# Half of a kernel's attention-probability tiles transposed as 32x32 blocks on VectorE and regrouped through DRAM

## The chip, the cores and the metric

The kernel runs on one core of one Trainium2 chip. The metric is the device time of one execution in microseconds (us). A core has a matrix engine (TensorE, in the profile PE, with its weight loads shown as PEld), VectorE (DVE), ScalarE (ACT), GpSimd (POOL) and SyncE (SP), which here only issues transfers (DMAs). Each engine executes its own instructions strictly in the order in which they stand in the program, and an instruction that waits for another engine holds back everything behind it on its own engine.

## The reference

A two-layer encoder trunk over 1024 tokens of width 1024, in float32. Layer 0 mixes with differential attention (8 heads, each the difference of two softmaxes of 64-wide queries and keys), layer 1 with latent attention (8 heads, scores from a 128-wide and a 64-wide part). Cut to what matters:

```python
# layer 0, per block of 128 queries
sc = jnp.einsum('bqhcd,bkhcd->bhcqk', qb, k) * scale
p = jax.nn.softmax(sc, axis=-1)
p = p[:, :, 0] - lam * p[:, :, 1]
o = jnp.einsum('bhqk,bkhd->bqhd', p, v)
# layer 1
sc = (einsum('bqhd,bkhd->bhqk', qn, k_nope) + einsum('bqhr,bkr->bhqk', qp, k_pe)) * scale
p = jax.nn.softmax(sc, axis=-1)
o = einsum('bhqk,bkhd->bqhd', p, v)
```

Around it stand an RMS norm, a conditioning shift, scale and gate, input projections, a SiLU gate, an output projection and a residual. The changed kernel computes the same.

## The kernel before

**Precision.** Every matrix product is made of three TensorE products (`mm3`, lines 186 to 188): an operand is split into a rounded part (`...h`, a cast on ACT) and the rest (`...l`, a subtraction on DVE or POOL), and the products high x high, high x low and low x high are added.

**Attention.** A head has 1024 queries, taken as 8 tiles of 128 queries; below, tiles are numbered from the start of a layer, 8 to a head. For one tile:

- Layer 0 (`q_tile`, L873): scores `s` of 128x1024 for c=0 and again for c=1, four matmuls of 128x512 each, into one of two PSUM buffers: c=0 always gets one of them, c=1 the other. `softmax_part` takes the row maximum on DVE (`nm`, L404) and the exponential on ACT (`e`, L406): for c=0 into a tile `e`, for c=1 in place. DVE then forms e0 + z*e1 (L879 to L881). Only after that is the buffer of c=1 free for the next tile.
- Layer 1 (`scores1`, L1703): ten matmuls of 128x512 into one of two buffers used in turn, `nm`, `e`. A buffer is free once its exponential is done.

The product with V needs the probabilities with the keys on the partitions, so each `e` is transposed: four TensorE transposes of 128x128 write one PSUM bank `tr` (L387), ACT rounds it into `pth` (L389), DVE writes the rest `ptl` (L390); twice per tile (kh = 0, 1). Two tiles t = 0, 1 form a query pair `qp`, four pairs to a head. When both are transposed, 24 matmuls of 128x256 (`pv`) add up the output of the pair. `after_scores` and the class `Tail` set the program order: a tile's first half is transposed after the scores of the next tile, its second half among the scores of the one after that, and `pv` follows there.

**Filling.** Between these pieces stand steps of other work for TensorE (`acc`): one step is three matmuls of 128x512 of the projections that the next heads need. `FILL0` and `FILL1` say how many steps stand at each place. Their weights come through `wraw` (DMA), `wh` (ACT) and `wl` (POOL, L235); the rotated queries and keys through DMAs `rp_sw` and POOL (L331, L336, L350 to L359).

**What sets the order.** The program text is the wish; a scheduler places the instructions of each engine and moves one ahead of another where it holds that the other is not ready. What it made is fixed in the program, and the order listings below show it. All DMAs are issued by SP, in one queue.

Of the kernel before, what the change touches and what calls it, by code (L numbers as in the profile page):

```python
# [40 lines left out]
FILL0 = ((1, 2, 1, 1, 1, 0), (1, 1, 1, 1, 1, 1)) * 3 + ((1, 2, 1, 1, 1, 0), (1, 1, 1, 1, 1, 0))  # L41
FILL1 = ((1, 0, 1, 0), (0, 1, 0, 0)) * 4
# [49 lines left out]
def trunk(ctx: ExitStack, tc: tile.TileContext, A, out):  # L92
# [303 lines left out]
    def alloc_pt(ap_):  # L396
        pth = [ap_.tile([P, 4, 2 * P], F32R, name="pth", tag="pt", bufs=6) for _ in range(2)]
        ptl = [ap_.tile([P, 4, 2 * P], F32R, name="ptl", tag="pt", bufs=6) for _ in range(2)]
        return pth, ptl
# [463 lines left out]
    def q_tile(h, half, ti, zz, ep, mid=lambda i: None):  # L863
# [5 lines left out]
        for c in range(2):  # L869
# [4 lines left out]
            with tc.issue_after(combined[-1]) if c == 0 and combined else nullcontext():  # L874
                es.append(softmax_part(None if c else ep, s_ps, zs[c], 1 if ep is a0a else 3))
# [34 lines left out]
    def finish(o, y, l, h, half, dst, ap_, dgs):  # L910

        if dst is None:
            b, rb = bcast_rows(ap_, y, "osq", 4)
# [60 lines left out]
    class Tail:  # L974
# [12 lines left out]
        def pv(self, kh):  # L987
# [3 lines left out]
            if kh == 0:  # L991
                if qp == 0:
                    c["vt"] = load_v(c["pool"], c["l"], c["h"])
                if qp % 2 == 0:
                    c["o_"] = bank("pv", "pv")
                    c["open"](qp // 2)
# [4 lines left out]

    tails, hooks = [None, None], []

# [15 lines left out]
    def after_scores(fill, n):  # L1019

        prev, last = tails
        if last:
            last.turn(0)
        fill(n)
        if prev:
            prev.pv(0)
        fill(n + 1)
        new = hooks[:]
        if prev:
            prev.pv(1)  # L1030
        fill(n + 2)
        for f in new:
            hooks.remove(f)
            f()

    def attn0(h, fills, extra=None, late=None):
# [10 lines left out]
        ctx_ = dict(pool=a0b, l=0, h=h, open=lambda half: None, close=close)  # L1047
        for qp in range(4):
            half = qp // 2
            if qp % 2 == 0:  # L1050
                zz = first.pop(0) if first else sm.tile([P, 4], F32, name="zz")
            for t in range(2):
# [13 lines left out]
                if first:  # L1066
                    e0 = first.pop()
                else:
                    e0 = q_tile(h, half, (qp * 2 + t) % 4, zz, a0b, mid)
                    fill(2)  # L1070
                    after_scores(fill, 3)
                side.tick()
                tails[:] = [tails[1], Tail(qp, t, e0, zz, ctx_)]
# [171 lines left out]
    tail0 = attn0(NH - 1, lambda i: FILL7[i] if i < Z_LAST else (0,) * 6, extra0, late0)  # L1245
    mk.clear()
# [30 lines left out]
    def group0(gi, fulls):  # L1277
# [3 lines left out]
        def chunk(k):  # L1281
            if gi == 1:
                h1[k][1] = xt2k("h1h"), xt2k("h1l")
                h1f[k] = ut(f"h1f{k}", dt=F32)
# [19 lines left out]
    def ut(name, spare=False, dt=F32R):  # L1304
        return up.tile([P, HF], dt, name=name, tag="us" if spare else "u", bufs=4 if spare else 20)
# [4 lines left out]
    wp = pool(stw, "wp1", side="right")  # L1310
    stv = ExitStack()
# [31 lines left out]
    def combos():  # L1343
# [5 lines left out]
        for k in range(4):  # L1349
# [19 lines left out]
            split_t(3, k, t3_, (ut("t3h"), ut("t3l")))  # L1369
# [228 lines left out]
    cqput = lora(3, CQ, qag, QL, lambda: ut("cqr", dt=F32), lambda: ut("cq"), 1)  # L1598
# [88 lines left out]
    def scores1(h, half, ti, zz):  # L1687
# [18 lines left out]
        return softmax_part(ap, s_ps, zz[:, ti : ti + 1])  # L1706
# [3 lines left out]
    def attn1(h, fills, extra=None, late=None):  # L1710
# [14 lines left out]
        ctx_ = dict(pool=ap, l=1, h=h, open=open_, close=close)  # L1725
        for qp in range(4):
            half = qp // 2
            if qp % 2 == 0:
                zz = first1.pop(0) if first1 else sm.tile([P, 4], F32, name="zz1")
            for t in range(2):  # L1730
# [7 lines left out]
                if first1:  # L1738
                    e = first1.pop()
                else:  # L1740
                    e = scores1(h, half, ti, zz)
                    fill(0)
                    after_scores(fill, 1)
                tails[:] = [tails[1], Tail(qp, t, e, zz, ctx_)]
# [18 lines left out]
    for n, steps in V1_AT:  # L1763
        for tt in v1_left[:n]:
            v1_tile(tt, 1, ap, "pt", 6)
# [9 lines left out]
    for tt in v1_left:  # L1775
        v1_tile(tt, 1, ap, "pt", 6)
    stv.close()
    ap2 = pool(st5, "attn1b")
# [36 lines left out]
    tail1 = attn1(NH - 1, lambda i: (0, 0, 0, 0), extra1, late1)  # L1815
    mk.clear()
# [129 lines left out]
```

## Time and profile before

| | us |
|---|---|
| median of 3 runs | 1431.51 (1429.72 to 1432.22) |
| the profiled execution, its own time | 1429.47 |
| its span in the trace | 1427.7 |
| busy: PE, DVE, ACT, POOL | 1396.7, 903.3, 743.3, 603.7 |

The profiled execution took 1.8 us more than its span, and 2.0 us less than the median. The span runs from the first to the last recorded instruction. The granted TensorE clock was 0.997 over the run. Layer 0's attention lies at about 150 to 690 us, layer 1's at about 960 to 1340 us.

### The profile page before, as it was taken

How to read it: one execution, taken by the hardware profiler on the slowest of the kernel's cores; microseconds unless marked ns; L12 is line 12 of the kernel's file. 1: busy time of each engine (PE TensorE's matmuls, PEld its weight loads, DVE VectorE, ACT ScalarE, POOL GpSimd, SP SyncE). 2: the span in 40 equal slices, each digit the busy share in tenths (PEclk: the TensorE clock that was granted, in tenths of full speed). 3: DMA queues.
4: the chain of work that ended last, by engine and by line, in shares of the span. 5: the costliest groups of instructions: out<-in, count | busy, mean ns of one | idle time of the engine just before them, and what ended most of it. 6: DMA issues, size and time to landing. Idle time of an engine off the chain costs nothing.

```text
span 1427.7 us, 20748 instructions
## 1 busy us (share of the span) xinstructions
PE 1396.7 (98%) x7478; PEld 1167.8 (82%) x7478; DVE 903.3 (63%) x1366; ACT 743.3 (52%) x1318; POOL 603.7 (42%) x483
## 2 busy tenths in 40 slices
PE   9999899999999999998999999999999999999997
PEld 7778688888888887887788788887888888888886
DVE  7756786767777767677435876255566555555355
ACT  6623375666565656566343644345455454555442
POOL 4415164656464646453561244412241331413562
PEclk9999999999999999999999999999999999999999
DMA  9777723233332333236663132465334532336663
GB/s 350 252 231 231 243 69 95 84 103 82 96 98 88 94 92 89 89 96 224 240 200 125 52 104 82 146 191 167 113 115 115 135 101 81 99 96 215 217 209 138
DMA packets 128473, 201.64 MB, mean 141 GB/s; under 512 B 17777, under 2 KB 54769, under 8 KB 128370
## 3 DMA queue, kind: packets, MB, share of 16 engines
q1 hardware_dynamic: 128370, 200.31, 45.6%
q8 instruction: 59, 0.97, 0.3%
q14 instruction: 44, 0.36, 0.1%
HBM read 131.11 MB, written 45.55 MB: 124 GB/s over the span
## 4 chain that ended last, share of the span: by engine, by line
PE 80%; DVE 6%; DMA 5%; issue 3%; ACT 3%; POOL 2%; SPq 1%; ACTq 0%; POOLq 0%; DVEq 0%
PE s L1703 9%; PE acc L188 8%; PE acc L186 8%; PE acc L187 8%; PE tr L387 7%; PE s L873 7%; PE oacc L186 4%; PE oacc L188 4%; PE oacc L187 4%; PE pv L187 4%; PE pv L188 4%; PE pv L186 4%; DVE ada L444 2%; PE zacc L186 1%; PE zacc L188 1%
## 5 line engine op out<-in xcount | busy, mean ns | idle before, releaser
L389 ACT CAST pth<-tr 128x512 fp32r<-128x512 f32 x256 | 150.2, 587 | 280.4 <-PE tr L387 277.2
L404 DVE TENSOR_REDUCE nm<-s 128x1 f32<-128x1024 f32 x192 | 233.9, 1219 | 72.7 <-PE s L873 66.3
L390 DVE TENSOR_TENSOR ptl<-tr,pth 128x512 fp32r<-128x512 f32 x256 | 176.1, 688 | 136.6 <-ACT pth L389 136.1
L235 POOL TENSOR_TENSOR wl<-wraw,wh 128x512 fp32r<-128x512 f32 (+2 forms) x82 | 101.3, 1237 | 234.6 <-ACT wh L234 212.5
L387 PE MATMUL tr<-ident,e 128*128 128x128 f32 x1024 | 154.6, 273 | 4.4 <-DVE ptl L390 4.2
L387 PEld LDWEIGHTS tr<-ident,e 128*128 128x128 f32 x1024 | 120.7, 140 | 46.1 <-DVE ptl L390 22.6
L406 ACT ACTIVATE e<-s,nm 128x1024 f32<-128x1024 f32 x128 | 143.6, 1122 | 24.8 <-DVE nm L404 24.4
L186 PE MATMUL acc<-h0h,wh 128*128 128x512 f32 x360 | 151.2, 420 | 2.5 <-DVE v_hl L366 1.7
L186 PE MATMUL pv<-pth,vt 128*128 128x256 f32 x512 | 147.4, 288 | 0.0
L187 PE MATMUL pv<-ptl,vt 128*128 128x256 f32 x512 | 145.8, 285 | 0.0
L188 PE MATMUL pv<-pth,vt 128*128 128x256 f32 x512 | 144.7, 283 | 0.0
L188 PE MATMUL acc<-h0h,wl 128*128 128x512 f32 x360 | 142.9, 397 | 0.1
L187 PE MATMUL acc<-h0l,wh 128*128 128x512 f32 x360 | 142.0, 394 | 0.0
L1118 POOL TENSOR_TENSOR wol<-wor,woh 128x512 fp32r<-128x512 f32 x64 | 84.7, 1343 | 83.7 <-ACT woh L1117 79.5
L186 PEld LDWEIGHTS pv<-pth,vt 128*128 128x128 f32 x512 | 97.3, 190 | 3.1 <-ACT pth L389 0.5
L187 PEld LDWEIGHTS pv<-ptl,vt 128*128 128x128 f32 x512 | 97.5, 190 | 2.8
L188 PEld LDWEIGHTS pv<-pth,vt 128*128 128x128 f32 x512 | 97.7, 191 | 0.1
L873 PE MATMUL s<-ks,qa 128*128 128x512 f32 x256 | 82.7, 403 | 5.2 <-DVE e L881 2.7
L336 POOL TENSOR_TENSOR rp_sw<-rp_sw,sinT 128x512 f32<-128x512 f32 x42 | 55.3, 1316 | 71.1 <-DMA rp_sw<-rp_raw 69.5
L881 DVE SCALAR_TENSOR_TENSOR e<-s,z,e 128x1024 f32<-128x1024 f32 x64 | 82.1, 1283 | 2.1
L331 POOL TENSOR_TENSOR rp_r<-rp_raw,cosT 128x512 f32<-128x512 f32 x38 | 49.7, 1307 | 77.3 <-ACT rp_raw L326 44.0
L873 PE MATMUL s<-ks,qb 128*128 128x512 f32 x256 | 81.1, 396 | 0.5 <-DMA qb<-qb 0.5
(624 smaller groups left out, 3355.5 us busy)
## 6 DMA issues: line engine op xcount, KB each, us to landing
ada<-in_ada_ss SPq DMA_DIRECT2D x32, 512.0 KB, 6.8
wraw<-in_w_s SPq DMA_DIRECT2D x64, 256.0 KB, 2.8
vS<-v_hl SPq DMA_DIRECT2D x32, 512.0 KB, 4.8
vt<-vS SPq DMA_DIRECT2D x32, 512.0 KB, 4.5
wor<-in_w_out SPq DMA_DIRECT2D x64, 256.0 KB, 3.5
rp_sw<-rp_raw SPq DMA_DIRECT2D x168, 64.0 KB, 2.0
bc_s<-bc_d SPq DMA_DIRECT2D x30, 256.0 KB, 4.2
oS<-bc_s SPq DMA_DIRECT2D x30, 256.0 KB, 2.6
```

Of the source, the lines that this page charges most:

```text
L186: PE.matmul(psum, ah, bh, start=first, stop=False)
L187: PE.matmul(psum, ah, bl, start=False, stop=False)
L188: return PE.matmul(psum, al, bh, start=False, stop=last).ins
L235: sub = (lo_on or (V if pair_of else G)).tensor_sub(l_[:, :n], raw[:, :n], f32v(h_[:, :n]))
L387: PE.transpose(tr[:, j, :], p[:, kt * P : (kt + 1) * P], ident)
L389: mk["S"] = S.copy(pth[kh][:, :, dst], tr).ins
L390: mk["V"] = V.tensor_sub(ptl[kh][:, :, dst], tr, f32v(pth[kh][:, :, dst])).ins
L404: mk["V"] = V.reduce_max(nm, s_ps, axis=AX.X, negate=True).ins
L406: mk["S"] = S.activation(e, s_ps, AF.Exp, bias=nm, scale=1.0, accum_out=zs).ins
L873: PE.matmul(s_ps[:, kc * HF : (kc + 1) * HF], src[:, c, ql], KS[h][kc][:, c, :], start=fst, stop=not fst)
L1118: in_turn(G.tensor_sub(lo, raw, f32v(hi)))
L1703: PE.matmul(s_ps[:, kc * HF : (kc + 1) * HF], lhs, rhs(kc), start=i == 0, stop=i == 4)
```

## The change

In heads 0 to 6 of both layers the pairs qp = 0 and 2 are no longer transposed on TensorE. DVE transposes each 32x32 block of `e` in place of it (`Mate.move`, one instruction per tile into `eT`), a DMA stores `eT` in DRAM (`pS`), and four DMAs per pair fetch it back so that every block lands on its partitions (`Mate.fetch`, into `pr`, rows of 1 KB). ACT rounds `pr` into `pth` with two casts of 128x1024, DVE and POOL subtract one half of `ptl` each (`Mate.split`). The other pairs, and all of head 7, go through TensorE as before. In the program text the fetch stands two tiles after the pair's second tile, the split three, its `pv` four; the `pv` of the other pairs stands one tile later than before. `FILL0` and `FILL1` place the filling steps anew, with the same number of steps. Buffers: `pt` 8 instead of 6, `e` 2 instead of 3, one `pr`, `eT` 1 (layer 0) or 2 (layer 1); to make room some tiles of the stage between the layers (`uv`, `V1_BUF`) move to other pools.

```diff
-FILL0 = ((1, 2, 1, 1, 1, 0), (1, 1, 1, 1, 1, 1)) * 3 + ((1, 2, 1, 1, 1, 0), (1, 1, 1, 1, 1, 0))
-FILL1 = ((1, 0, 1, 0), (0, 1, 0, 0)) * 4
+FILL0 = ((1, 2, 1, 1, 1, 1), (1, 1, 1, 0, 1, 1), (1, 1, 1, 1, 1, 0), (1, 2, 1, 1, 1, 1), (1, 2, 1, 1, 1, 1), (1, 1, 1, 0, 1, 1), (1, 1, 1, 1, 1, 0), (1, 2, 1, 1, 1, 0))
+FILL1 = ((1, 1, 0, 0), (0, 0, 1, 0), (0, 0, 1, 0), (1, 1, 0, 0)) * 2
+V1_BUF = (("vt", 3), ("qps", 4)) * 2 + (("vt", 3),)
...
+    class Mate(Tail):
...
+        def move(self, t, e):
+            eT = self.c["pool"].tile([P, D], F32, name="eT", tag="eT", bufs=self.c["nT"])
+            mk["V"] = V.transpose(eT.rearrange("p (c k j) -> p c k j", c=4, j=32), e.rearrange("p (k c i) -> p c k i", c=4, i=32)).ins
+            SP.dma_start(self.store[t], eT)
+
+        def fetch(self):
+            self.raw = self.c["pool"].tile([P, 2, 4, 256], F32, name="pr", tag="pr", bufs=1)
+            src = self.store.rearrange("t (a i) (c r) -> c i t a r", a=4, c=4)
+            for c_ in range(4):
+                SP.dma_start(self.raw[c_ * 32 : c_ * 32 + 32], src[c_])
+
+        def split(self):
+            pth, ptl = self.pt = alloc_pt(self.c["pool"])
+            r = self.raw.rearrange("p t a (k j) -> p k (t a) j", j=32)
...
+            for kh in range(2):
+                S.copy(view(pth[kh]), r[:, kh * 4 : kh * 4 + 4])
+            for kh, eng in enumerate((V, G)):
+                eng.tensor_sub(view(ptl[kh]), r[:, kh * 4 : kh * 4 + 4], view(f32v(pth[kh])))
...
+        if mate:
+            mate.move(t, e)
+            if t:
+                prep.setdefault(n + 2, []).append(mate.fetch)
+                prep.setdefault(n + 3, []).append(mate.split)
+                due.setdefault(n + 4, []).extend([lambda: mate.pv(0), lambda: mate.pv(1)])
...
+        elif t and wait is not None:
+            due.setdefault(n + 2 + wait, []).extend([lambda: tail.pv(0), lambda: tail.pv(1)])
...
+            mate = Mate(qp, ctx_) if qp % 2 == 0 and not late else None
```

**Where instructions moved, place 1: PE in layer 0, second tile of the third head** (tile 17). `s` are the scores (one name per buffer use: s_2840 is c=1 of tile 17, s_2894 and s_2909 are c=0 and c=1 of tile 18), `acc` the filling steps, `tr` a transpose, `pv` the product with V. Before:

```order
L873 MATMUL s_2913<-ks_2387,qb_2641 128x512
L873 MATMUL s_2913<-ks_2505,qb_2641 128x512
L186 MATMUL acc_2924<-h0h0_0_102,wh_2830 128x512
L187 MATMUL acc_2924<-h0l0_0_103,wh_2830 128x512
L188 MATMUL acc_2924<-h0h0_0_102,wl_2831 128x512
L387 MATMUL tr_2932<-ident_79,e_2824 128x128 x4
L186 MATMUL acc_2924<-h0h1_0_106,wh_2830 128x512
L187 MATMUL acc_2924<-h0l1_0_107,wh_2830 128x512
L188 MATMUL acc_2924<-h0h1_0_106,wl_2831 128x512
L186 MATMUL pv_2782<-pth_2768,vt_2407 128x256
L187 MATMUL pv_2782<-ptl_2770,vt_2407 128x256
```

and after the change:

```order
L874 MATMUL s_2840<-ks_2336,qb_2572 128x512
L874 MATMUL s_2840<-ks_2447,qb_2572 128x512
L874 MATMUL s_2894<-ks_2336,qa_2571 128x512
L874 MATMUL s_2894<-ks_2447,qa_2571 128x512
L874 MATMUL s_2894<-ks_2336,qb_2572 128x512
L874 MATMUL s_2894<-ks_2447,qb_2572 128x512
L187 MATMUL pv_2858<-pth_2728,vt_2385 128x256
L874 MATMUL s_2909<-ks_2336,qa_2571 128x512
L874 MATMUL s_2909<-ks_2447,qa_2571 128x512
L874 MATMUL s_2909<-ks_2336,qb_2572 128x512
L874 MATMUL s_2909<-ks_2447,qb_2572 128x512
L188 MATMUL pv_2858<-ptl_2730,vt_2385 128x256
```

The scores of tile 18 now stand directly behind those of tile 17, with one `pv` matmul between them; the filling and the `pv` of more than one tile have moved behind them.

**Place 2: DVE in layer 1, around the first tile of the fourth head** (tile 24). `nm` is the row maximum of the scores named behind the arrow, `ptl` on `tr` a subtraction of the TensorE path, `ptl` on `pr` (L1031) one of the new path, `gwh` a product for the gate. Before (s1_11021 are the scores of tile 24, s1_11069 those of tile 25, and the next `pv` uses ptl_10973 and ptl_10974):

```order
L404 TENSOR_REDUCE nm_11039<-s1_11021 128x1
L390 TENSOR_TENSOR ptl_10973<-tr_11053,pth_10971 128x4x128
L444 ISA gwh_9682,gcol_9044<-gwh_9682,c2h_9680,vec_88 128x512
L444 ISA gcol_9044 128x1
L444 ISA gwh_9683,gcol_9044<-gwh_9683,c2h_9681,gcol_9044 128x512
L444 ISA gcol_9044 128x1
L1643 TENSOR_TENSOR kn_l_11064<-acc_11043,kn_h_11063 128x512
L390 TENSOR_TENSOR ptl_10974<-tr_11076,pth_10972 128x4x128
L404 TENSOR_REDUCE nm_11087<-s1_11069 128x1
```

and after (s1_10707 are the scores of tile 23, s1_10755 those of tile 24):

```order
L405 TENSOR_REDUCE nm_10718<-s1_10707 128x1
L405 TENSOR_REDUCE nm_10773<-s1_10755 128x1
L445 ISA gwh_9522,gcol_8879<-gwh_9522,c2h_9520,vec_88 128x512
L445 ISA gcol_8879 128x1
L1031 TENSOR_TENSOR ptl_10527<-pr_10482,pth_10525 128x1024
L445 ISA gwh_9523,gcol_8879<-gwh_9523,c2h_9521,gcol_8879 128x512
L445 ISA gcol_8879 128x1
L391 TENSOR_TENSOR ptl_10509<-tr_10544,pth_10507 128x4x128
L391 TENSOR_TENSOR ptl_10508<-tr_10569,pth_10506 128x4x128
```

The subtraction of the new path (pair of tiles 16 and 17) stands behind the row maximum of tile 24, where before every `ptl` of the coming `pv` stood ahead of the next row maximum.

**Place 3: PE at the same point of layer 1, after the change:**

```order
L1768 MATMUL s1_10755<-kps0_6933,qpb_10040 128x512
L1768 MATMUL s1_10755<-kps1_6934,qpb_10040 128x512
L187 MATMUL pv_10615<-pth_10525,vt_10533 128x256
L188 MATMUL pv_10615<-ptl_10527,vt_10533 128x256
L189 MATMUL pv_10615<-pth_10525,vt_10533 128x256
L388 MATMUL tr_10569<-ident_79,e_10500 128x128 x4
L187 MATMUL pv_10615<-pth_10525,vt_10533 128x256
```

and before, behind the scores of tile 25:

```order
L1703 MATMUL s1_11069<-kps0_7101,qpb_10224 128x512
L1703 MATMUL s1_11069<-kps1_7102,qpb_10224 128x512
L186 MATMUL acc_11102<-cq_9369,wh_11047 128x512
L187 MATMUL acc_11102<-cq_9370,wh_11047 128x512
L188 MATMUL acc_11102<-cq_9369,wl_11048 128x512
L186 MATMUL pv_10989<-pth_10971,vt_10753 128x256
L387 MATMUL tr_11095<-ident_79,e_11041 128x128 x4
L187 MATMUL pv_10989<-ptl_10973,vt_10753 128x256
```

The second `pv` matmul, which needs ptl_10527 of place 2, now stands right behind the scores of tile 24; before, it stood behind a filling step and its `ptl` was made earlier.

111 lines of the change are left out of this document (71 added, 40 removed).

## The prediction

> **What bounds the kernel now.** I read the page from the top: the engines' shares, then the chain of work that ended last.
>
> ```profile
> span 1427.7 us, 20748 instructions
> PE 1396.7 (98%) x7478; PEld 1167.8 (82%) x7478; DVE 903.3 (63%) x1366; ACT 743.3 (52%) x1318; POOL 603.7 (42%) x483
> ...
> PE 80%; DVE 6%; DMA 5%; issue 3%; ACT 3%; POOL 2%; SPq 1%; ACTq 0%; POOLq 0%; DVEq 0%
> PE s L1703 9%; PE acc L188 8%; PE acc L186 8%; PE acc L187 8%; PE tr L387 7%; PE s L873 7%; PE oacc L186 4%; PE oacc L188 4%; PE oacc L187 4%; PE pv L187 4%; PE pv L188 4%; PE pv L186 4%; DVE ada L444 2%; PE zacc L186 1%; PE zacc L188 1%
> ```
>
> TensorE is the bound, and its transposes (tr, L387) are on the chain. A share over the run says little, so next the stretches (columns: stretch, length, then busy us and count for PE, PEld, DVE, ACT, POOL, clock, DMA share, GB/s; one from layer 0's attention, one from layer 1's) and what PE waited for.
>
> ```profile
> 400.00:500.00 100.00, 99.93 (x561) 84.87 (x560) 74.25 (x104) 62.22 (x110) 57.65 (x48) 1.00 0.35 95
> 1200.00:1300.00 100.00, 100.00 (x613) 86.09 (x612) 54.63 (x72) 51.64 (x93) 25.27 (x21) 1.00 0.43 124
> ```
>
> ```profile
> PE tr L387 <- DVE ptl L390: 4.2, 6, 1.4
> PE s L873 <- DVE e L881: 2.7, 3, 1.0
> PE s L873 <- ACT e L406: 2.1, 1, 2.1
> ```
>
> In both layers PE is busy throughout at the full clock and waits for almost nothing, so a matmul removed there is time removed, as long as the new order doesn't make PE wait. That condition is the whole question.
>
> **What is removed.** The timeline around one group of four transposes:
>
> ```profile
> 426.92 0.39 PE L188 MATMUL acc<-h0h,wl 128*128 128x512 f32 x1
> ...
> 427.15 0.60 PE L387 MATMUL tr<-ident,e 128*128 128x128 f32 x4
> ...
> 427.50 0.48 PE L186 MATMUL acc<-h0h,wh 128*128 128x512 f32 x1
> ...
> 427.82 0.39 PE L187 MATMUL acc<-h0l,wh 128*128 128x512 f32 x1
> ...
> 428.05 0.40 PE L188 MATMUL acc<-h0h,wl 128*128 128x512 f32 x1
> ...
> 431.17 0.28 PE L187 MATMUL pv<-ptl,vt 128*128 128x256 f32 x1
> ...
> 431.29 0.28 PE L188 MATMUL pv<-pth,vt 128*128 128x256 f32 x1
> ```
>
> Durations overlap; starts count. A 128x512 matmul takes 428.05-427.82 = 0.23, a 128x256 one 0.12. From 426.92 to 427.82 lie 0.90, of which two matmuls are 0.46: four transposes take 0.44. Two layers x 7 heads x 2 pairs x 2 tiles x 2 halves = 112 groups go: **-49.3 us**. About half of the 4.2 us that transposes waited for ptl goes too: **-2.1**. The other matmuls stay in number.
>
> **What the engines beside it get.** Groups that price the new work (after the bar: busy us, mean ns of one), from the page:
>
> ```profile
> L389 ACT CAST pth<-tr 128x512 fp32r<-128x512 f32 x256 | 150.2, 587 | 280.4 <-PE tr L387 277.2
> L404 DVE TENSOR_REDUCE nm<-s 128x1 f32<-128x1024 f32 x192 | 233.9, 1219 | 72.7 <-PE s L873 66.3
> L390 DVE TENSOR_TENSOR ptl<-tr,pth 128x512 fp32r<-128x512 f32 x256 | 176.1, 688 | 136.6 <-ACT pth L389 136.1
> ...
> L881 DVE SCALAR_TENSOR_TENSOR e<-s,z,e 128x1024 f32<-128x1024 f32 x64 | 82.1, 1283 | 2.1
> ```
>
> and one each from the groups of ACT and POOL by shape, and from the view of line 340 (ns min/median/max):
>
> ```profile
> L1270 ACT ACTIVATE tjunk<-xfull 128x1024 bf16<-128x1024 f32 x8 | 8.5, 1058 | 7.5 <-DVE xfull L1166 7.3
> ...
> L235 POOL TENSOR_TENSOR wl<-wraw,wh 128x512 fp32r<-128x512 f32 x62 | 82.4, 1330 | 100.5 <-ACT wh L234 99.1 <-PE acc L188 1.2
> ...
> L340 DVE TENSOR_TENSOR rp_r<-rp_r,rp_sw x42: 675/682/2020, 99.7 to 1242.6; 128x512 f32<-128x512 f32 x42
> ```
>
> - DVE loses 112 ptl of 0.69 (77 us). It gains 28 subtractions of 128x1024, taken as L881 at 1.3 (36 us). They read SBUF twice while POOL does the same, and L340, which does so too, ranges from 0.68 to 2.02 (median 0.68), so they may reach 2.6. It also gains 56 block transposes. No row shows one; by the nearest, between 0.69 (128x512) and twice the 1.28 of 128x1024, I take 1.25 (70 us), as both rows of 128x1024 are near it. Net +29 us of 903; DVE has 26 us free in each 100 of its fullest stretch, so it is hidden, except where a wait stands on it (below).
> - ACT loses 112 casts of 0.59 (66 us) and gains 56 of 128x1024: between 1.06 (L1270) and 2x0.59, so about nothing.
> - POOL gains 28 subtractions of 2x1.33 = 2.66 us (75 us), with 42 free in each 100; behind one stand the weight halves wl and the rotations.
> - SP issues 56 stores and 112 fetches more, 58.7 MB. Each store waits for a transpose, each fetch for both stores and for the one pr buffer; behind them in SP's queue stand weight loads, rp_sw and vt. The moves of vt and of the tiles between the layers I cost at nothing: they are loaded earlier, or as early, under the same PE work.
>
> **What the new order adds: waits of PE.** In layer 0 the buffer of c=1 is freed by a chain. One turn of it, in the timeline:
>
> ```profile
> 422.10 0.62 PE L873 MATMUL s<-ks,qa 128*128 128x512 f32 x2
> ...
> 422.55 0.63 PE L873 MATMUL s<-ks,qb 128*128 128x512 f32 x2
> ...
> 423.85 1.22 DVE L404 TENSOR_REDUCE nm<-s 128x1 f32<-128x1024 f32 x1
> ...
> 425.36 1.09 ACT L406 ACTIVATE s<-s,nm 128x1024 f32<-128x1024 f32 x1
> ...
> 426.60 0.16 DVE L879 RECIPROCAL z<-z 128x1 f32<-128x1 f32 x1 [0.94 <-ACT s L406]
> ...
> 427.11 1.28 DVE L881 SCALAR_TENSOR_TENSOR e<-s,z,e 128x1024 f32<-128x1024 f32 x1
> ...
> 428.44 0.30 PEld L873 LDWEIGHTS s<-ks,qa 128*128 128x128 f32 x2 [0.21 <-DVE e L881]
> 428.52 0.66 PE L873 MATMUL s<-ks,qa 128*128 128x512 f32 x2
> ```
>
> From start to start 6.4 us, of which the row maximum stood 0.6 behind other DVE work: the chain alone takes **5.8**. Between two c=1 scores PE must have that much work, or it waits. I added up the PE rows of the order listing by the three prices above. Before, there are mostly 6.2 to 10.4 us between them, and all shortfalls add up to 3.8, most in the last head, near the 4.8 that the waits show, so the count can be trusted. After, the order is lumpy: in place 1 only 1.96 us stand between s_2840 and s_2909, so PE waits 3.9. Such lumps stand at tiles 9 to 10, 17 to 18, 25 to 26 and 41 to 42, with shortfalls (both buffers) of 3.4, 3.9, 3.3 and 1.8 us; the last head has 6.6, the rest 3.4. Together 22.4, less the 3.8: **+18.6**. In layer 1 the like count gives **+0.9**.
>
> At each lump more is queued. pv needs the new ptl, which DVE makes behind e (L881): 1.3 against 0.92 of PE work, 0.4 each, **+1.6**. And POOL's subtraction (2.66) and the wl behind it (1.33) stand ahead of the next filling step: some 2 us at three lumps, **+6**.
>
> In layer 1, places 2 and 3: PE's second pv matmul stands right behind the scores of tile 24, and its ptl on DVE behind the row maximum of these scores. PE waits for 1.22 + 1.3 + 0.2 of gaps = 2.7, less the 0.12 that it has to do. The order has this at six of the 14 pairs: four cost 2.6 to 2.7, one 2.1, and the one shown, with a gate product and a ptl for the next transposes behind it, 4.7: **+17.3**.
>
> **The sum.** -49.3 - 2.1 + 18.6 + 0.9 + 1.6 + 6 + 17.3 = -7.0 on 1429.47, so 1422.5 for a run like the profiled one. That one lay 2.0 below the median; with it, **1424** as the median. Most of what the transposes give back goes into new waits.
>
> **Do the data come in time?** Rows for the transfers (KB each, us to landing):
>
> ```profile
> wraw<-in_w_s SPq DMA_DIRECT2D x64, 256.0 KB, 2.8
> vS<-v_hl SPq DMA_DIRECT2D x32, 512.0 KB, 4.8
> vt<-vS SPq DMA_DIRECT2D x32, 512.0 KB, 4.5
> ...
> rp_sw<-rp_raw SPq DMA_DIRECT2D x168, 64.0 KB, 2.0
> ...
> x1S<-xfull SPq DMA_DIRECT2D x8, 512.0 KB, 3.4
> ...
> cosT<-tabS SPq DMA_DIRECT2D x4, 128.0 KB, 2.7
> ```
>
> A store of 512 KB takes about 3.4 (x1S). A fetch, four DMAs of 256 KB, lies between 2.8 (all at once) and 11.2 (one after another); I take 6. With a single pr buffer, a pair's turn in layer 1 is: POOL's subtraction of the pair before (2.7), fetch 6, cast 1.2, subtraction 1.3 = 11 us, against 21 us of PE work from one pair's pv to the next. In layer 0 there are about 31. So it is hidden by 10 us.
>
> vS, which writes in short pieces (the rearranged store of `store_v`), is hardly slower than vt, which reads straight. By this the regrouping in the fetch, in rows of 1 KB, should cost little. [...]
>
> **Rivals.**
> - *Fewer waits.* The chain is hidden better than counted, above all where DVE and ACT catch up while PE waits. Against it: the count fits the trace of before. If half of the 44.4 us are real, about 1400. Chance 0.15.
> - *The gain is eaten up.* DVE subtractions slowed by POOL (1.3 more at 28 places), the seams of head 7, SP's queue: 4 to 10 us more, and it ends within 0.2% of 1431.5. For it: every new wait is one that the scheduler's order did not foresee. Chance 0.18.
> - *Slower: the fetch comes late.* If it takes over 15 us instead of 6, as DMAs wait in SP's queue behind one another, layer 1's turn exceeds its 21 us, and ACT, DVE and POOL all stand at the split with row maxima and weights behind it. At 16.5 it costs 1.5 us at 13 pairs, 20 us: 1444. For it: SP is one queue. Against it: the rows above. Chance 0.13.
> - *Slower: DVE is too slow.* A block transpose of 2.5 us stands between row maxima in layer 1, where tiles follow at 2.5 to 3.0 us; 1.25 more at one tile of each pair in layer 1 and at the lumps is some 25 us: 1447. Chance 0.10.
> - *The regrouping is slow.* If rows of 1 KB moved no faster than the small pieces of rp_sw (64 KB in 2.0), the 1024 KB of a fetch, one after another, would take 32 us, 17 beyond the 15 that have room, at 28 pairs: some 1900. For it: nothing of this shape and size is in the trace. Against it: vS beside vt. Chance 0.02. [...]
>
> **How the numbers follow.** My forecast, 1424 with a range of its own of 1410 to 1428, has 0.42. Faster by over 0.2% (2.9 us, about what a measurement of this kernel can tell from no change) are it and the first rival: 0.57. Within: 0.18. Slower: 0.25. The range leaves out the lower part of the first rival and the worst of the slow ones: 1394 to 1446.
>
> **What would show it.** In the profile after: 576 transposes on L388; L874 waiting for e (L882) with 15 to 25 us in all, in waits of 2 to 4; pv (L188) waiting for the new ptl (L1031) with 10 to 20, most in layer 1; wl with a few; STREAM_TRANSPOSE at 1.2 to 1.4 us; pr landing within 6 us. Waits of ACT for pr would show the late fetch, DVE near 90% in layer 1 the slow transposes, no long waits of PE the first rival. The forecast is wrong if PE's waits add up to under 25 or over 60 us.

## The result and the profile after

| | before | after |
|---|---|---|
| median, us (4 runs each) | 1430.62 | 1546.43 |
| ratio, 95% interval | | 1.0811 (1.0792 to 1.0831) |
| profiled execution, its span | 1429.47, 1427.7 | 1545.08, 1543.3 |

The kernel became 116 us slower; the forecast was 1424, and the range ended at 1446. The page after, its first part and the chain:

```profile
span 1543.3 us, 20214 instructions
PE 1409.3 (91%) x7030; PEld 1159.7 (75%) x7030; DVE 947.2 (61%) x1338; ACT 740.2 (48%) x1262; POOL 681.0 (44%) x511
...
PE 47%; DVE 13%; issue 12%; DMA 10%; POOL 8%; ACT 6%; SPq 3%; POOLq 0%; ACTq 0%; DVEq 0%
```

448 matmuls are gone (7478 to 7030), and yet PE's busy time has grown by 12.6 us. Its share fell from 98% of the span to 91% and from 80% of the chain to 47%. The two stretches of 100 us that were full before:

```profile
400.00:500.00 100.00, 90.07 (x465) 74.22 (x465) 63.56 (x85) 52.41 (x88) 52.20 (x40) 0.98 0.51 134
1200.00:1300.00 100.00, 88.01 (x484) 73.51 (x483) 57.70 (x68) 46.17 (x76) 36.05 (x25) 0.97 0.64 171
```

PE stands idle for 10 to 12 of each 100 us, no other engine is near full, and the granted clock is no longer 1.00. What PE waited for (us in total, times, longest):

```profile
PE acc L189 <- POOL wl L236: 24.1, 18, 3.3
PE pv L188 <- DVE ptl L1031: 20.8, 12, 3.6
PE s L874 <- DVE e L882: 18.3, 17, 4.1
PE tr L388 <- DVE ptl L391: 13.6, 12, 4.3
PE pv L187 <- ACT pth L1029: 7.9, 5, 2.6
PE ssq L959 <- ACT rp_raw L329: 5.3, 2, 3.7
PE s L1768 <- ACT e L407: 5.2, 7, 0.8
PE s L874 <- ACT e L407: 4.6, 6, 1.2
```

The time that no wait explains is in the clock. Around two waits that follow each other closely (0.97 us for e, 2.18 for the subtraction), in stretches of 3.41 us (columns as in the other windows; the third number from the end is the granted clock):

```profile
188.75:192.16 3.41, 2.68 (x12) 1.88 (x10) 2.06 (x4) 2.94 (x4) 0.00 (x0) 1.00 0.71 231
192.16:195.58 3.42, 1.29 (x5) 0.80 (x5) 3.42 (x3) 0.64 (x2) 3.19 (x2) 1.00 0.43 153
195.58:198.99 3.41, 3.12 (x14) 3.12 (x15) 3.12 (x4) 0.58 (x2) 1.38 (x1) 0.50 0.02 5
198.99:202.40 3.41, 3.41 (x31) 3.41 (x30) 2.49 (x5) 3.28 (x7) 0.00 (x0) 1.00 0.38 154
```

PE was busy for only 1.29 of the 3.42 us up to 195.58. In the next 3.41 us the clock is 0.50: 14 matmuls pass, where 31 do in the stretch behind (those of 128x256 start 0.21 us apart, and 0.12 behind it). So these waits were paid twice: once while they lasted, and again by up to 1.7 us (half of 3.41) after them. The records of the clock have 32 such stretches after, 2 before. PE's busy time in them was 93.5 us; at a clock of 0.50 I take half of it, **46.8 us**, as loss. With it the sum closes:

| us | before | after | difference |
|---|---|---|---|
| PE idle (span less busy) | 31.0 | 134.0 | +103.0 |
| lost to the half clock | 1.7 | 46.8 | +45.1 |
| PE busy, less that loss | 1395.0 | 1362.5 | -32.5 |
| span | 1427.7 | 1543.3 | +115.6 |

The new operations themselves are not the surprise. From the view by tile (ns min/median/max) and the page's DMA issues (KB each, us to landing):

```profile
L1012 DVE STREAM_TRANSPOSE eT<-e x56: 1226/1235/1247, 163.5 to 1380.4; 128x1024 f32<-128x1024 f32 x56
...
L1029 ACT CAST pth<-pr x56: 1034/1046/1066, 190.3 to 1403.0; 128x1024 fp32r<-128x1024 f32 x56
L1031 POOL TENSOR_TENSOR ptl<-pr,pth x28: 2325/2482/3355, 192.4 to 1404.2; 128x1024 fp32r<-128x1024 f32 x28
L1031 DVE TENSOR_TENSOR ptl<-pr,pth x28: 1205/1224/3065, 193.3 to 1403.2; 128x1024 fp32r<-128x1024 f32 x28
...
pS<-eT SPq DMA_DIRECT2D x56, 512.0 KB, 3.4
pr<-pS SPq DMA_DIRECT2D x112, 256.0 KB, 6.1
```

The forecast had 1.25, 1.06 to 1.18, 2.66, 1.3 and 3.4; the medians lie within 7% of it. The exception is the fetch, forecast at 6 us. The 6.1 of the last row is the time of one of its four DMAs; from the issue of the first to the landing of the fourth a fetch took 11.0 us at the median, 7.8 to 14.6, close to the upper end that the prediction gave (11.2, one after another).

### The profile page after: what moved, and what is told of

It is laid out like the page before. It is cut to its first block, busy times and chain, and to the rows that moved or that the text cites. A ratio compares the mean times of both kernels' runs of the same rounds, so it can differ in the third digit from the quotient of the medians.

```text
span 1543.3 us, 20214 instructions
## 1 busy us (share of the span) xinstructions
PE 1409.3 (91%) x7030; PEld 1159.7 (75%) x7030; DVE 947.2 (61%) x1338; ACT 740.2 (48%) x1262; POOL 681.0 (44%) x511
## 4 chain that ended last, share of the span: by engine, by line
PE 47%; DVE 13%; issue 12%; DMA 10%; POOL 8%; ACT 6%; SPq 3%; POOLq 0%; ACTq 0%; DVEq 0%
PE acc L189 5%; PE acc L187 5%; PE acc L188 4%; PE oacc L189 3%; PE oacc L188 3%; PE oacc L187 3%; PE s L1768 3%; PE tr L388 3%; DMA pr<-pS 3%; PE pv L188 2%; DVE nm L405 2%; PE pv L189 2%; PE pv L187 2%; PE s L874 2%; POOL wl L236 2%
## 5 line engine op out<-in xcount | busy, mean ns | idle before, releaser
L188 PE MATMUL pv<-ptl,vt 128*128 128x256 f32 x512 | 156.8, 306 | 23.2 <-DVE ptl L1031 20.8
L391 DVE TENSOR_TENSOR ptl<-tr,pth 128x512 fp32r<-128x512 f32 x144 | 98.8, 686 | 111.0 <-ACT pth L390 110.7
L390 ACT CAST pth<-tr 128x512 fp32r<-128x512 f32 x144 | 84.6, 587 | 169.8 <-PE tr L388 168.9
L187 PE MATMUL pv<-pth,vt 128*128 128x256 f32 x512 | 152.4, 298 | 13.0 <-ACT pth L1029 7.9
L1031 POOL TENSOR_TENSOR ptl<-pr,pth 128x1024 fp32r<-128x1024 f32 x28 | 75.4, 2694 | 187.0 <-ACT pth L1029 130.0
L189 PE MATMUL pv<-pth,vt 128*128 128x256 f32 x512 | 151.1, 295 | 0.0
L187 PEld LDWEIGHTS pv<-pth,vt 128*128 128x128 f32 x512 | 103.7, 203 | 19.8 <-ACT pth L1029 10.3
L388 PE MATMUL tr<-ident,e 128*128 128x128 f32 x576 | 96.1, 293 | 14.2 <-DVE ptl L391 13.6
L874 PE MATMUL s<-ks,qa 128*128 128x512 f32 x256 | 86.9, 420 | 23.0 <-DVE e L882 18.3
L189 PEld LDWEIGHTS pv<-pth,vt 128*128 128x128 f32 x512 | 104.2, 204 | 0.9
L189 PEld LDWEIGHTS acc<-h0h,wl 128*128 128x128 f32 x360 | 71.0, 197 | 40.2 <-POOL wl L236 25.2
L388 PEld LDWEIGHTS tr<-ident,e 128*128 128x128 f32 x576 | 72.6, 150 | 35.2 <-DVE ptl L391 23.2
L187 PEld LDWEIGHTS acc<-h0h,wh 128*128 128x128 f32 x360 | 71.9, 200 | 20.0 <-DVE v_hl L367 2.1
L874 PE MATMUL s<-ks,qb 128*128 128x512 f32 x256 | 83.9, 408 | 0.0
```

The costliest lines, as they stand in the source:

```text
L187: PE.matmul(psum, ah, bh, start=first, stop=False)
L188: PE.matmul(psum, ah, bl, start=False, stop=False)
L189: return PE.matmul(psum, al, bh, start=False, stop=last).ins
L388: PE.transpose(tr[:, j, :], p[:, kt * P : (kt + 1) * P], ident)
L390: mk["S"] = S.copy(pth[kh][:, :, dst], tr).ins
L391: mk["V"] = V.tensor_sub(ptl[kh][:, :, dst], tr, f32v(pth[kh][:, :, dst])).ins
```

## The experiments

### Which part of the change, which layer

`no_mate` keeps the buffers and moved tiles of the change alone; `l0_only` and `l1_only` have the new path in one layer.

```diff
 # no_mate: both layers; l0_only: layer 1 only; l1_only: layer 0 only. FILL0 or FILL1 of that layer as before
-            mate = Mate(qp, ctx_) if qp % 2 == 0 and not late else None
+            mate = None
-                settle(..., (0 if late else 1) if qp < 3 or not late else None)
+                settle(..., 0 if qp < 3 or not late else None)
```

> All heads transpose on TensorE again and the filling stands as before; only the buffers, pools and the moved loads of the change stay. If the loss comes from the new path and the order it makes: 1430 us, within 5 us of before, and the granted clock again 0.997. If two e buffers in place of three, or the moved tiles, were behind it: tens of us slower than before, up to 1546.

> The new path in layer 0 alone; layer 1 transposes on TensorE. Layer 0's attention grew from 531 to 611 us in the changed kernel. If each layer loses by its own waits: about 1431 + 79 = 1510 us, with most half-clock stretches (20 or more) still there. If the loss needs both layers (buffers or DMA shared): well under 1490.

> The new path in layer 1 alone. Layer 1's attention grew from 353 to 391 us in the changed kernel. If each layer loses by its own waits: about 1431 + 37 = 1468 us, with 7 or so half-clock stretches, layer 0 as before. My prediction had layer 1 by itself 6 us faster than before (24.6 removed, 18.2 of waits): 1425.

Measured: no_mate 1433.46, ratio 1.0023 (1.0012 to 1.0034); l0_only 1512.07 (82 us over before); l1_only 1467.34 (37 over). The buffers and moved tiles cost some 3 us, and the two layers add up: each loses by itself. That layer 1 alone would gain 6 us was wrong; it has 13 half-clock stretches, where 7 were expected.

### What a wait costs

Into layer 1 of the kernel before, where PE waits for almost nothing, waits of known place were put: two transposes of `ident`, VectorE operations that read them, a transpose that needs their result, and the scores behind it.

```diff
+    def gap():
+        ta = bank("tr", "ga", [P, 4, P])       # gap_mini: an acc bank
+        for j in range(2):
+            tc.keep_in_program_order(PE.transpose(ta[:, j, :], ident, ident))
+        V.tensor_copy(gj, ta[:, :2, :])
+        for _ in range(6):                     # gap_short: 1, gap_mini: 0
+            V.tensor_mul(gj, gj, gj)
+        tb = bank("tr", "gb", [P, 4, P])
+        return PE.transpose(tb[:, 0, :], gj[:, 1, :], ident).ins
...
-                    e = scores1(h, half, ti, zz)
+                    with tc.issue_after(gap()) if h in range(1, 7) and t in (1,) else nullcontext():   # short, mini: (0, 1)
+                        e = scores1(h, half, ti, zz)
```

> The kernel before, with 24 waits of TensorE put into layer 1 (heads 1 to 6, every second tile): two transposes, a chain of seven short VectorE operations that reads them, and a transpose that needs its result, with the scores behind it. Each wait should be about 2.5 to 3 us, some 65 us together, shown as waits of gb for DVE. If a long wait also halves the granted clock in the 3.41 us behind it, as the records of the changed kernel suggest: about 18 half-clock stretches, and some 1.7 us more for each, so the time is 95 to 100 us above before. If the clock has other causes: only the waits, some 65 to 70 us, at a clock of 0.997.

> The same with 48 waits of about 1.0 to 1.4 us (two VectorE operations in the chain, every tile of heads 1 to 6), some 55 to 65 us together. If the clock falls only when TensorE is idle for more than about half of a 3.41 us stretch: hardly any half-clock stretch (0 to 4), and the time is above before by the waits alone, 60 to 70 us. If any wait costs clock: as many us above the waits as in the kernel with the long ones.

> As gap_short, with one VectorE operation in the chain and the two transposes in an acc bank, so that nothing else is waited for: 48 waits of 1.0 to 1.4 us, some 60 us together. The two kernels with longer waits had half-clock stretches behind every 3.41 us in which TensorE was busy for less than 0.49. With waits this short no such stretch should arise: at most 5 half-clock stretches, a clock of 0.99 or more, and a time above before by the waits and the added transposes alone (60 to 80 us). If waits cost clock in proportion: some 25 half-clock stretches and 20 to 30 us more.

The waits of the three kernels (gap_long, gap_short, gap_mini in this order):

```profile
PE gb L1719 <- DVE gj L1717: 90.4, 24, 6.1
PE ga L1714 <- DVE ptl L390: 20.5, 18, 1.7
...
PE gb L1719 <- DVE gj L1717: 83.0, 48, 3.0
PE ga L1714 <- DVE ptl L390: 20.5, 24, 1.7
...
PE gb L1717 <- DVE gj L1715: 39.4, 48, 1.9
```

| | time, us | over before | PE idle, more than before | half-clock stretches in all | loss to the half clock, more than before | other PE time, more than before |
|---|---|---|---|---|---|---|
| gap_long, 24 waits of 3.8 | 1613.50 | 185 | 116.7 | 40 | 48.6 | 17.0 |
| gap_short, 48 of 1.7 | 1592.57 | 164 | 100.9 | 25 | 36.3 | 27.9 |
| gap_mini, 48 of 0.8 | 1499.49 | 69 | 39.8 | 2 | 0.0 | 27.8 |

The waits came out longer than designed in the first two (the transposes also waited for the tr bank). gap_long's expectation held in kind, but not in size (95 to 100 us over before were expected); gap_short did not stay under the bound, and its expectation failed. gap_mini gives the contrast, as expected: 48 waits of 0.82 us on average (the longest 1.9), and not one half-clock stretch beyond the 2 that the kernel before has. Here the short waits cost their own time; the longer ones cost clock as well: 2.0 us for each wait of 3.8 (48.6 / 24), 0.8 for each of 1.7 (36.3 / 48), none for those of 0.8. The other PE time holds the added transposes; it was not divided further.

All twenty traces of this study, cut into these stretches, say where the bound lies. Counted are stretches at full clock, and how many of them were followed by one at half clock:

```
PE busy, share of the 3.41 us     stretches    next one at half clock
below 0.44                              245          245
0.44 to 0.50                             54           31
0.50 to 0.54                             53            4
0.54 and above                         7876            5
```

So in these traces the bound lies between 0.44 and 0.54 of a stretch busy: PE idle for about half of it, 1.6 to 1.9 us, in one wait (those of 3.8 on average in gap_long) or in several that fall into the same stretch (the 0.97 and 2.18 above, which left 1.29 busy). The five at 0.54 and above are not explained.

### Is it TensorE's order?

In the forecast PE waited because of lumps in the scheduler's order. `pin` holds PE to the order of the text. The lines of this kernel and its relatives lie 13 below those of the changed kernel (L404 is L391, L1044 is L1031).

```diff
+            r = nc.tensor.matmul(*a, **k)                # transposes likewise
+            return tc.keep_in_program_order(r) if held_pe[0] else r     # on in heads 0 to 6 of both layers
```

> The changed kernel with the same operations, but TensorE's instructions in heads 0 to 6 of both layers held in the order of the program text, so that no scores are moved ahead of filling steps. If the lumps that the scheduler made are what TensorE waits for: the waits on e (L882) and on the subtraction (L1031) fall from 41 us to under 15, few half-clock stretches remain, and the time falls to 1400 to 1450 us. If the new work is too much for DVE, ACT, POOL or the transfers in any order: the waits only move to other places (wl, pth, ptl), and the time stays above 1500.

Measured: 1603.45, ratio 1.1216 (1.1194 to 1.1238): slower still. The theory fell in this form, and the trace shows why. The waits of layer 0, then of layer 1:

```profile
PE tr L106 <- DVE ptl L404: 83.0, 19, 8.4
PE s L101 <- DVE e L895: 4.5, 4, 2.7
...
PE tr L106 <- DVE ptl L404: 80.0, 15, 9.1
PE pv L101 <- DVE ptl L1044: 2.7, 1, 2.7
```

The waits for e, wl and the subtraction are nearly gone (4.5, 1.2 and 2.7 us), and one kind has taken their place, almost all of it at one tile in four (in layer 0 some 6 us idle on average at the first of four, 0.05 at the others). The timeline there:

```profile
181.37 0.60 PE L106 MATMUL tr<-ident,e 128*128 128x128 f32 x4
...
186.68 1.98 ACT L1042 CAST pth<-pr 128x1024 fp32r<-128x1024 f32 x2
188.56 0.58 ACT L403 CAST pth<-tr 128x512 fp32r<-128x512 f32 x1
188.64 1.25 DVE L1025 STREAM_TRANSPOSE eT<-e 128x1024 f32<-128x1024 f32 x1
...
189.81 2.35 DVE L1044 TENSOR_TENSOR ptl<-pr,pth 128x1024 fp32r<-128x1024 f32 x1
192.08 0.68 DVE L404 TENSOR_TENSOR ptl<-tr,pth 128x512 fp32r<-128x512 f32 x1
...
192.90 1.09 PE L106 MATMUL tr<-ident,e 128*128 128x128 f32 x4 [7.92 <-DVE ptl L404]
```

The one tr bank is written at 181.4 and needs two short operations (0.58 us on ACT, 0.68 on DVE) to come free. In ACT's queue the split's two casts stand ahead of the first, behind the next tile's exponentials; in DVE's the block transpose and the split's subtraction stand ahead of the second. The old path, of which half is left, waits behind the new one, and PE stands 7.9 us.

So the split was moved:

```diff
 # pin_s4; pin_s4p5 also: due n + 5, and pv of the other pairs one tile later
-                prep.setdefault(n + 3, []).append(mate.split)
+                prep.setdefault(n + 4, []).append(mate.split)
 # pin_s4k, pin_s4kv: as pin_s4, with these two in keep_in_program_order; pin_s4kv also (V, V)
                 S.copy(view(pth[kh]), r[:, kh * 4 : kh * 4 + 4])
                 eng.tensor_sub(view(ptl[kh]), r[:, kh * 4 : kh * 4 + 4], view(f32v(pth[kh])))
```

> As pin (TensorE in the order of the text), with the split one tile later, behind the TensorE path's own casts and subtractions in the text. In pin all idle time stood at one tile in four, where the split's casts and subtraction stand in ACT's and DVE's queues ahead of those that free the tr bank (163 us of waits for ptl L404). If that collision is the cause: these waits fall to under 40 us, and the time from 1603 to below 1470; at no waits, 1431.5 - 49.3 = 1382. If the engines beside are simply too full in any order: the waits move to pv for the subtraction (L1044) or to e, and the time stays above 1520.

> As pin_s4, and the pv of the new path's pairs one tile later too (that of the others as well), so that pv does not wait for the split. If the collision at the split was the whole cause: 1385 to 1440 us, under pin_s4 by what pv waited there. If the engines beside are too full: above 1520.

> As pin_s4, with the split's casts and subtractions held in the order of the text on ACT, DVE and POOL too, ahead of the tile's own exponentials. pin_s4 waited 76 us at pv for the split, whose casts stood behind the exponential of c=1. If the place in the queues is the cause: these waits fall below 30 us and the time from 1537 to 1470 to 1500. If the engines are too full there in any order: e, nm or wl take over and the time stays within 15 us of 1537.

> As pin_s4k with both subtractions on VectorE. In pin VectorE's subtraction took 2.35 us beside POOL's against 1.22 alone, so two on VectorE alone cost it about as much as one beside POOL's, and POOL is free for wl. Expected: VectorE's subtractions at 1.22, at or below the time of pin_s4k by up to 20 us. If VectorE's length matters most: slower than pin_s4k.

| | us | ratio, interval | what PE waited for now |
|---|---|---|---|
| pin_s4 | 1536.91 | 1.0753 (1.0728 to 1.0778) | tr for ptl 163 to 16; pv for the split 76 |
| pin_s4p5 | 1563.04 | 1.0929 (1.0887 to 1.0972) | layer 0: e 26, wl 22; layer 1: pv for the split 40 |
| pin_s4k | 1602.30 | 1.1199 (1.1178 to 1.1219) | pv for POOL's subtraction 62, for ACT's casts and DVE's 86 |
| pin_s4kv | 1539.11 | 1.0768 (1.0748 to 1.0789) | pv for ACT's casts and DVE's 79, e 17 |

pin_s4 shows that the collision was the cause of the 163 us of waits for the bank. But none of the four reaches the time that was hoped for: the waits come back at the next reader. The times of pin_s4 and pin_s4p5, above 1520, are those expected of engines that are too full in any order, so these four don't refute that reading. pin_s4kv against pin_s4k shows one price: with both subtractions on VectorE 63 us less, where 20 at most were expected.

`sub_vv` does that in the changed kernel itself (`enumerate((V, V))`):

> The changed kernel with both subtractions on VectorE and none on GpSimd. In the changed kernel TensorE waited 24 us for wl, which stands behind the 2.7 us subtraction on POOL. If that is its cause: waits for wl fall below 8 us and VectorE's subtractions, no longer beside POOL's, stay at 1.22; the waits for ptl (L1031) may rise by up to 15; time 1515 to 1540. If POOL is not the cause: wl waits stay near 24 us.

Measured: 1524.17, ratio 1.0654 (1.0636 to 1.0672), 22 us better than the changed kernel. The time is as expected, the reason isn't: PE's waits for wl are 22.6 us as against 24.1, so the subtraction on POOL, to which the forecast put them, is not what makes them. Of the 25 us that the span is shorter (1518.5), 15.3 are loss to the half clock (31.5, not 46.8).

### Taking the path out, part by part

These kernels leave work out: `no_path` has none of the new path, and the 28 pairs' pv reads four fixed tiles; `no_split` has the block transposes and stores, `split_only` the casts and subtractions, of a fixed pr; `free_split` does everything, but its split reads the constant tables and so waits for no fetch. no_path and no_split also go back to 6 `pt` buffers.

```diff
 # no_path and no_split: split()
+            self.pt = fixed[id(p_)]            # four tiles, written once from cosT
 # no_path and split_only: move()
-            mk["V"] = V.transpose(eT..., e...).ins
-            SP.dma_start(self.store[t], eT)
 # no_path and no_split: fetch() empty; split_only: fetch()
+            self.raw = fixed[id(p_)]           # one pr, written once
 # free_split: split()
-            r = self.raw.rearrange("p t a (k j) -> p k (t a) j", j=32)
+            r = [x_.rearrange("p (a k j) -> p k a j", k=4, j=32) for x_ in (cosT, sinT)]
```

> The changed kernel without the new path's work: no block transposes, stores, fetches, casts or subtractions; the 28 pairs' pv reads four fixed tiles. TensorE's work is that of the changed kernel. It asks what the 448 transposes are worth when nothing takes their place. If TensorE is the bound and only the replacement's work costs: 1430.5 - 49.3 = 1381, between 1375 and 1400 us, with few half-clock stretches. If the lumps of filling and pv alone make TensorE wait: above 1430.

> As no_path, but with the block transposes and the stores (no fetch, casts or subtractions). If the split (casts and subtractions between the tiles' own work) is what makes TensorE wait: within 20 us of no_path. If the block transposes on VectorE between row maxima are: 60 us or more above it.

> As no_path, but with the split's casts and subtractions of a fixed pr (no block transposes and no transfers). If the split is the cause: 80 us or more above no_path, near the 1546 of the changed kernel. If it is the sum of everything: between.

> The changed kernel with all of its work, transfers too, but the split's casts and subtractions read the constant tables in place of pr, so nothing waits for a fetch and the order no longer hangs on one. If what costs is that the split depends on the transfers (by which the scheduler sets it late and moves scores ahead of filling): near split_only, 1425 to 1445 us. If the transfers themselves cost (SP's queue, load on the DMA engines): within 30 us of the changed kernel's 1546.

| | us | ratio, interval | step |
|---|---|---|---|
| no_path | 1382.39 | 0.9679 (0.9661 to 0.9696) | the transposes' worth: -47 |
| no_split | 1385.74 | 0.9700 (0.9678 to 0.9721) | block transposes and stores: +3 |
| split_only | 1427.99 | 0.9994 (0.9981 to 1.0007) | split alone: +46 over no_path |
| free_split | 1507.29 | 1.0532 (1.0509 to 1.0554) | fetches, and all parts together: +76 more |
| changed kernel | 1546.43 | 1.0811 (1.0792 to 1.0831) | split depends on its fetch: +39 more |

The gain was there, as large as forecast, with PE idle for 33.1 us of its span, about as before. The split alone gives nearly the whole gain back. In split_only and in no_path PE waited (split_only first):

```profile
PE tr L388 <- DVE ptl L391: 23.9, 16, 3.0
PE s L874 <- DVE e L882: 11.4, 8, 2.7
...
PE tr L388 <- DVE ptl L391: 1.0, 3, 0.6
PE s L874 <- DVE e L882: 5.9, 7, 2.0
```

Of the 32.8 us that PE is idle longer (65.9 against 33.1), 22.9 are waits of the old path's transposes for their bank and 5.5 waits for e. Neither reads anything of the split. The waits of pv for the split itself are 5.1 us, those for wl are the same in both (1.7 and 1.6). Another 8.1 us went to the half clock. What was expected of split_only if the split were the whole cause, 80 us or more, did not come: it is one part of several.

The largest step is that of the parts together; free_split fell between its two expected times (1425 to 1445, or within 30 us of 1546). In it, PE waited for wl as nowhere else:

```profile
PE acc L189 <- POOL wl L236: 50.1, 23, 6.5
...
POOL ks L351 <- ACT ks L349: 79.1, 13, 12.9
POOL qb L359 <- ACT qa L357: 55.0, 11, 13.3
...
SPq L1013 <- DVE eT L1012: 93.2, 27, 9.5
...
POOL o L917 <- DMA bc_s<-bc_d: 37.9, 7, 8.2
```

One of these waits in the timeline:

```profile
428.41 0.62 ACT L349 CAST ks<-rp_r 64x512 fp32r<-64x512 f32 x1
...
429.17 1.26 POOL L351 TENSOR_TENSOR ks<-rp_r,ks 64x512 fp32r<-64x512 f32 x1 [1.35 <-ACT ks L349]
...
430.51 1.27 POOL L352 TENSOR_TENSOR ks<-rp_r,ks 64x512 fp32r<-64x512 f32 x1
...
431.86 1.27 POOL L332 TENSOR_TENSOR rp_r<-rp_raw,cosT 128x512 f32<-128x512 f32 x1
...
433.07 1.27 POOL L236 TENSOR_TENSOR wl<-wraw,wh 128x512 fp32r<-128x512 f32 x1
...
434.39 0.80 PE L189 MATMUL acc<-h0h,wl 128*128 128x512 f32 x1 [5.36 <-POOL wl L236]
```

wl stands in POOL's queue behind the subtractions of the rotated keys, and these wait for ACT's cast of the keys. Twelve of the waits for wl are longer than 2 us, 43 of the 50.1 us together. At ten of them POOL's last wait ahead of wl is for such a cast of the keys or queries (ks, qa), at one for the split's cast, at one for a result of VectorE. These two rows of POOL are 16.3 and 12.5 us in no_path, 19.0 and 13.1 in split_only.

A second candidate is SP: its one queue has stood 93.2 us at stores that wait for eT, and POOL waited 37.9 us for rows `bc_s` that SP fetches (4.8 in no_path). But none of the twelve has such a wait of POOL in the 15 us before it, and in the changed kernel the SP and bc_s rows are larger (115.5 and 79.3) while the waits for wl are half (24.1). So this is not what makes wl late there, as far as POOL's waits tell. What makes the casts late isn't shown; a kernel with the stores in another queue was not tried, nor the fetches alone, so how the 76 us divide stays open.

The last step, +39, is not the time of waiting for the data alone: ACT waited for pr 8.9 us in all. With nothing to wait for, pv's waits for the split (20.8 + 7.9 + 1.6 us in the changed kernel) are gone in free_split, and those for wl are 26 us larger.

### Attempts at a better version

`s4p5_vv` puts the split at n + 4 and pv at n + 5, with both subtractions on VectorE, PE not held. `l1_even` does so in layer 1 alone, with

```diff
-FILL1 = ((1, 1, 0, 0), (0, 0, 1, 0), (0, 0, 1, 0), (1, 1, 0, 0)) * 2
+FILL1 = ((1, 1, 1, 0), (1, 1, 1, 0), (0, 0, 0, 0), (0, 0, 0, 0)) * 2
```

> The changed kernel with the split and pv one tile later, both subtractions on VectorE, and the scheduler free on all engines. If time between fetch and pv was what was short: the waits of pv (L1031) fall from 22 us to under 8, and the time to 1470 to 1500. If the engines' full tiles are the cause wherever the split stands: 1510 to 1550.

> An attempt at a version that beats both: the new path in layer 1 alone, split and pv one tile later, both subtractions on VectorE, and layer 1's filling moved to the two tiles of four that have no pv; layer 0 as before. In s4p5_vv layer 1's attention took 7 us more than before, of which 4 are the buffers alone (no_mate). If the evened filling takes half of the remaining waits: 1420 to 1430 us. If the doubled pv and the split still meet: 1435 to 1445.

Measured: s4p5_vv 1486.97, ratio 1.0409 (1.0370 to 1.0448): the waits of pv for the subtraction fell from 20.8 to 7.2, as expected of more time, and those for wl rose to 33.1. The time is in the expected range. l1_even 1448.41, ratio 1.0128 (1.0106 to 1.0149), 18 us over before and above both expected times. No version that does all the work of the new path beat the kernel before.

## Why the prediction was wrong

- **What is removed, -49.3: right.** no_path lies 47 below before.
- **The prices of the new operations: right at the median**, as shown above; VectorE's subtractions took 1.55 us on average, as eight of the 28 took 1.58 to 3.07.
- **The fetch: mis-sized, 11.0 us instead of 6.** By the prediction's own reckoning a pair's turn in layer 1 is then 16 us of 21, so there still was room, and at 25 of the 28 pairs the casts began 1.7 us or more after the fetch had landed. At three pairs of layer 1 ACT did wait for pr, 8.9 us in all, at two of them with the second store issued 17 and 18 us after its block transpose; PE waited 3.9 us for the split there. So the late fetch came, at 3 pairs of 28, and is worth little by itself.
- **The regrouping was not slow.** One DMA of 256 KB in rows of 1 KB landed in 6.1 us at the median, issued with three others, a plain load of the same size (wraw) in 3.1. The 32 us for a fetch did not come: it took 11.0.
- **The two waits that were counted from the order: right in sum, half of it by luck.** For e in layer 0 18.6 more were forecast; the rows for s L874 (18.3 and 4.6) are 18.1 over the 4.8 of before. But the four lumps have 8.9 us (12.4 forecast) and the last head 1.9 (6.6), while 12.0 lie elsewhere (3.4), the longest of them 4.1 at tile 39. For pv behind the new ptl 1.6 in layer 0 and 17.3 in layer 1 were forecast; it is 6.6 and 14.1. In layer 1 the mechanism is the one that was forecast: four waits of 2.7 to 3.6 stand right behind the scores of a tile, the one of places 2 and 3 with 3.3 (4.7 forecast).
- **"So it is hidden, except where a wait stands on it" failed.** The sum put 24.9 us on the split: 1.6 + 17.3 for pv, which needs what the split makes, and 6 for wl, the one thing that it saw standing behind it, on POOL. It counted nothing for what stands behind it on VectorE and ScalarE. But the split is a burst, twice in a head of eight tiles, and in the traces each engine works its queue in order (after the change DVE started the nine instructions of place 2 as listed, at 1176.43 to 1186.17 us): what stood behind the burst was late. In the timeline of pin ACT's cast of tr starts at 188.56, where the split's casts end (188.66), and DVE's ptl at 192.08, where the split's subtraction ends (192.16). split_only prices the split alone at 46 us, and there 22.9 are waits for the old path's bank and only 5.1 waits of pv for the split. In the changed kernel tr waits 13.6 us for ptl (2.1 forecast) and pv 7.9 for the split's casts (0). The waits for wl are 24.1 (6), and not for the reason that was forecast, as sub_vv shows. I counted the waits of two chains in PE's order and took the other engines' queues as all but empty. PE's idle time grew by 103.0 us, against 44.4 - 2.1 = 42.3. By the prediction's own sign, over 60 us of waits, the forecast is wrong.
- **A term was missing: the clock.** "At the full clock" was taken for a property of the kernel, and the sum has no term for it; in these traces it is one of PE not waiting (PE idle for 31.0 us and 2 half-clock stretches before, 134.0 and 32 after). It cost 45.1 us. The trace of before had it, in the one place where PE waited long:

```profile
153.20:156.61 3.41, 1.25 (x5) 0.75 (x5) 3.41 (x7) 1.65 (x4) 0.00 (x0) 1.00 0.94 253
156.61:160.03 3.42, 3.42 (x8) 2.70 (x9) 3.40 (x8) 1.09 (x3) 0.00 (x0) 0.50 0.97 325
```

  I had counted waits of about 2 to 5 us at ten places or more (four lumps in layer 0, six pairs in layer 1). By gap_short and gap_long one of that kind loses 0.8 to 2.0 us of clock, an estimate of 8 to 20 us on top for my own waits alone. The forecast would have been 1432 to 1444, no change or slower instead of faster.
- **The rest.** PE's busy time without the clock's loss fell by 32.5, in no_path (1348.1 less 5.0) by 51.9. So 19 us more lie in the changed kernel's busy rows; what they are isn't shown. The sum closes with it: from -7.0 forecast to +115.6 measured are 60.7 us of idle time, 45.1 of clock and 16.8 that the busy time fell less than the 49.3.
- **The rivals.** Of "fewer waits" the opposite came. "The gain is eaten up" had DVE slowed by POOL and SP's queue at 4 to 10 us, far too little. "DVE is too slow" had the sign, but its block transpose took 1.24 us, not 2.5; "the fetch comes late" had the sign too, and is shown at three pairs only.

## What to carry to other kernels

When work left an engine that was never idle, the price of its replacement here was not its busy time against the others' free time, but what it delayed in each in-order queue at the tile in which it fell; count there, for every queue, the transfers' too. A saving of 1.76 us per pair (49.3 / 28) is lost to a single PE wait of that length, and some of it a second time at the half clock (0.8 us for each wait of 1.7 in gap_short). A kernel that leaves the new work out altogether tells in one run whether the gain exists, and two or three partial ones tell which part spends it.

## What the runs showed of the hardware

- In the twenty traces the granted clock followed PE's activity in stretches of 3.41 us: below 0.44 busy, half clock in the next one, 245 times of 245; from 0.44 to 0.54, 35 times of 107; at 0.54 and above 5 times of 7876. In gap_mini 48 waits of 0.82 us on average added no half-clock stretch to the 2 of before.
- VectorE's subtraction of 128x1024 took 1.22 us at the median. In the changed kernel POOL's subtraction ran beside all but one of the 28: 20 still took 1.21 to 1.23 us, eight took 1.58 to 3.07, and POOL's own took 2.33 to 3.36. With none on POOL (sub_vv) 50 of 56 took 1.18 to 1.23, and the other six, beside other work of POOL, 1.39 to 2.31. So beside POOL's it can be slow, but mostly wasn't; the 2.35 in the timeline of pin is one of eight such there.
- VectorE transposed the 32x32 blocks of a 128x1024 f32 tile in 1.23 to 1.25 us, 56 times.
